# The last group of down products of a two-layer trunk, emitted from a written list: other places for weight blocks, additions and single residual tiles on VectorE

## The chip, the cores and the metric

The kernel runs on one core of one Trainium2 chip. The metric is the device time of one execution in microseconds (us); the time of the kernel before is the median of three runs. Durations and start times inside the kernel come from one profiled execution, whose own time and span are given below.

## What is computed

Two layers of a hybrid encoder on 512 tokens of width 1024, float32. Each layer is a token mixer (layer 0: differential attention, layer 1: chunked gated linear attention) with a memory cross-attention beside it, an output projection, and a gated MLP with a causal depthwise convolution. The change touches the end of the MLP, its down projection, and the way from there to the next layer:

```python
def conv_ffn(h, w_up, conv_w, conv_b, w_down):
    u = h @ w_up
    c = lax.conv_general_dilated(u, conv_w[:, None, :].astype(u.dtype), ...) + conv_b
    a, g = jnp.split(c, 2, axis=-1)
    return (jax.nn.silu(g) * a) @ w_down

for i in range(DEPTH):
    ...
    h = rms_norm(x, ffn_norm[i])
    x = x + conv_ffn(h, w_up[i], conv_w[i], conv_b[i], w_down[i])
```

The hidden width D_FF is 2816 and the output width 1024.

## The kernel before

**Number format.** Every float32 product is made of three matmuls: an operand is split into a high part (a cast) and a low part (the difference), and high x high, high x low and low x high are summed. For a weight block ScalarE makes the high part (tile whi) and VectorE the low part (tile wlo); there are five buffers of each (WB = 5). Raw weights arrive by DMA from SyncE's queue into six buffers.

**The down projection** runs in three groups of 3, 4 and 4 hidden blocks (`GROUPS`), each over two column halves c = 0, 1 of the output. It is a Winograd-like scheme of seven products instead of eight for a 2 x 2 block matrix: a11, s1, a12, s2, s4, s3, a22, where s1 to s4 are sums of weight blocks that VectorE forms (`sum_weights`, L251 to L264). `DOWN` (L34) lists the 14 products of a group in their order; I number them 0 to 13 by that list. Function `step` (L1161) emits one product on TensorE: 4 hidden blocks x 2 output tiles x 3 matmuls = 24 matmuls into one of the PSUM banks lg, tp, mm. Function `add` (L1179) follows: one VectorE addition of the bank onto two residual tiles, halved over tokens (t = 0 or 1). Products that go on in the same bank (for c = 0: a11, s2, s3, a22 in lg, and s1, s4 in tp) have to wait until the addition before has read it, since the bank is read as a running sum.

**Weight blocks.** `weights` (L305) hands out the next block of the plan. `prefetch(i)` (L298) makes all blocks that fit the five buffers when product i is the oldest one in use; with one product per step it makes one block. `make_sum` (L266) makes a block: the cast on ScalarE (L272), the weight sum that the next product needs (L251 to L264), and the low part on VectorE (L274). A block whose buffer is still being read waits for the step that reads it.

**Finished tiles.** `done(c, f, t)` (L1183) calls `finish` (L1236) for the two tiles of a pair once their additions are in. In layer 0 `finish` calls `settle` (L1071): ScalarE scales the tile into a high part (L315) and squares it (L429 or L1080), VectorE makes the low part (L318) and adds the square to a running sum (L431 or L1081); then the tile is stored to DRAM. For the last four tiles (n = 4 to 7) this is done by token halves. In layer 1 `finish` only stores the tile to the output.

**The last group** (L1194 to L1232) starts with the first three hidden blocks of products 0, 1 and 2, and adds the fourth block of each after that, because that hidden block is finished last.

**What comes after layer 0's group.** The first projection of layer 1's mixer (`gemm`, L329, called at L852; its weights are pieces gm0 and gm1 of 272 columns) takes the finished tiles in the order 0, 1, 2, 3, 6, 7, 4, 5 (`GM`, L38), token blocks 2 and 3 first, then 0 and 1. Between these two halves TensorE forms the sum of squares (L437), which needs all tiles, for the row scales of the layer. The weight blocks of the projection after it (g0) are made beside this.

**Who sets the order.** TensorE follows program order everywhere. Inside `down` (L1292) ScalarE, VectorE and GpSimd do too. Everything else, SyncE's queue among it, and the work before and behind `down`, is placed by the scheduler of the language, which can put such an instruction between two of the ordered ones. `follow` (L323) reads a written list like `ORDER` (L48): each entry is a letter, a number, and for some a bank, and calls the function of that letter.

Of the kernel before, what the change touches and what calls it, by code (L numbers as in the profile page):

```python
# [33 lines left out]
DOWN = ((0, "a11"), (0, "s1"), (0, "a12"), (0, "s2"), (0, "s4"), (0, "s3"), (1, "a11"), (0, "a22"),  # L34
        (1, "s1"), (1, "s2"), (1, "a12"), (1, "s3"), (1, "s4"), (1, "a22"))
K8 = tuple(range(KT))
C4 = tuple(range(4))
GM = (0, 1, 2, 3, 6, 7, 4, 5)  # L38

PASS = ([[(c, (0, 1, 2)) for c in C4], [(c, (3, 6, 7, 4, 5)) for c in C4]],  # L40
        [[(c, (0, 1, 2, 6, 7)) for c in (0, 1, 2)] + [(3, (0, 1, 2))],
         [(c, (3, 4, 5)) for c in (0, 1, 2)] + [(3, (6, 7, 3, 4, 5))]])
# [23 lines left out]
def _pieces():  # L66
# [3 lines left out]
    def piece(key, name, i, ks, *ranges):  # L70
        plan.append((key, name, i, ks, ranges))

    for l in range(2):
# [9 lines left out]
        else:  # L83
# [3 lines left out]
            for c in range(5):  # L87
                piece(("g", c), w, 0, K8, (512 * c, min(512 * c + 512, 2304)))
        for i, part in enumerate(PASS[l]):
            for c, ks in part:  # L90
# [69 lines left out]
def trunk(ctx, tc, head_d, x_t, mem_t, wpack, cols_a_d, cols_d, conv_d, gate_d, rel_bias, diff_lambda, consts, onehot, out):  # L160
    nc = tc.nc
    mm = nc.tensor.matmul
# [10 lines left out]
    def bank(tag):  # L173
        return ps.tile([128, 512], F32, name=f"ps_{tag}", tag=tag)
# [17 lines left out]
    def blk(b, w=128):  # L192
        return slice(w * b, w * b + w)
# [13 lines left out]
    def tables(name):  # L207
        tc.keep_in_program_order(A.preload_act_table_set(name))
# [71 lines left out]
    def make_piece(raws=None, between=None):  # L280
        key = plan[len(made)][0]
        if key[0] == "d":
            made.append(make_sum(key))
            return
        parts = []
        for i, (_, _, kk, _, w) in enumerate(blocks[len(made)]):
            n = len(kk)
            raw = load_raw(raw_tile(), n * w) if raws is None else raws[i]
            hi, lo = (wp.tile([128, WTILE], F32R, name=t, tag=t, bufs=WB) for t in ("whi", "wlo"))
            if between is not None and i == 3:  # L290
                between()
            split_weights(slice(0, n * w), raw, hi, lo, len(made) == 2)
            parts += [(hi[:, blk(j, w)], lo[:, blk(j, w)]) for j in range(n)]
        made.append(parts)
# [3 lines left out]
    def prefetch(i):  # L298
        size = lambda j: 1 if plan[j][0][0] == "d" else len(blocks[j])
        by_block = plan[i][0][0] in "ud"  # L300
        while len(made) <= i or (len(made) < len(plan) and (
                sum(map(size, range(i, len(made) + 1))) <= WB if by_block else len(made) < i + 2)):
            make_piece()
# [19 lines left out]
    def follow(order, steps):  # L323
        for entry in order.split():
            op, n, tag = entry[0], entry[1:].rstrip("tsl"), BANKS.get(entry[-1] if len(entry) > 1 else "")
            steps[op](int(n), **({} if tag is None else {"tag": tag}))
# [98 lines left out]
    first = [bank("mm"), bank("mm"), bank("sm"), bank("sm")]  # L425
# [24 lines left out]
    with tc.tile_pool(name="ini", bufs=1) as ip, tc.manual_schedule(engines={E.Activation, E.DVE, E.Pool, E.SP}):  # L450
# [7 lines left out]
        p = bank("tp")  # L458
# [45 lines left out]
        for k in range(KT):  # L504
# [15 lines left out]
            for b, i in sorted(todo, key=lambda bi: bi[1]) if k == 0 else todo:  # L520
                xp, w = terms[i]
# [562 lines left out]
    def out_proj(l, mix, part, acc, late=None):  # L1084
        got, kk = {}, dict(PASS[l][part])
        turns = cycle(("mm", "mm", "sm", "sm") if late is not None else ("mm", "sm") if acc else ("mm",))

        def unit(n, i):
            c, ks = n // 2, kk[n // 2]
            if i == 0:  # L1090
                if c not in got:
                    got[c] = weights(("o", l, part, c))
                got["p", n] = bank(next(turns))
            p = got["p", n]
            product(p, got[c], n % 2, [mix[k] for k in ks], (i,))
            if i == len(ks) - 1:
                update(n, p, None if acc is None else (lambda k: c_ffn(l, k)), acc)

        def give(units):
            for u in units:  # L1100
                F.add(0.65, lambda u=u: unit(*u))
        units = [(2 * c + n, i) for c, ks in PASS[l][part] for n in range(2) for i in range(len(ks))]
        if late is None:
# [5 lines left out]
    def ffn(pool, l, acc):  # L1109
# [47 lines left out]
        def down(g, mids, finish):  # L1157
            last, ks = len(mids) - 1, tuple(range(len(mids)))
            parts, banks, first, last_group = {}, {}, used[0], g + 1 == len(GROUPS)

            def step(c, tag, w, m, ks=ks, start=False, more=True):  # L1161
                if (c, w) not in parts:
                    parts[c, w] = weights(("d", l, g, c, w), more)
                elif more:
                    prefetch(first + more)
                if start:
                    banks[c, tag] = bank(tag)
                p = banks[c, tag]
                hi, lo = parts[c, w]
                for k in ks:  # L1170
                    mh, ml = mids[k][m]
                    for n in range(2):
                        o, ws = p[:, blk(n, 256)], slice(256 * k + 128 * n, 256 * k + 128 * n + 128)
                        terms = (hi, mh), (hi, ml), (lo, mh)
                        for i, (a, b) in enumerate(terms):
                            mm(o[:, ::-1], a[:, ws], b[:, ::-1], start=start and (k, n, i) == (0, 0, 0), stop=k == last and i == 2,  # L1176
                               skip_group_check=True)

            def add(c, tag, f, t):  # L1179
                x = xpair[2 * c + f][:, :, blk(t, 256)]  # L1180
                V.tensor_add(x, x, banks[c, tag].rearrange("p (n s) -> p n s", n=2))  # L1181

            def done(c, f, t=None):  # L1183
                for n in range(2):
                    finish(4 * c + 2 * f + n, t)
            if not last_group:
                step(0, "lg", "a11", "b11", start=True)
                add(0, "lg", 0, 0)
                step(0, "tp", "s1", "t1", start=True)
                add(0, "tp", 1, 1)  # L1190
                step(0, "mm", "a12", "b21", start=True)
                add(0, "mm", 0, 0)
            else:
                step(0, "lg", "a11", "b11", ks[:-1], True)  # L1194
                step(0, "tp", "s1", "t1", ks[:-1], True, False)
                step(0, "mm", "a12", "b21", ks[:-1], True, False)
                step(0, "lg", "a11", "b11", ks[-1:], more=False)
                add(0, "lg", 0, 0)
                step(0, "tp", "s1", "t1", ks[-1:], more=1)
                add(0, "tp", 1, 1)  # L1200
                step(0, "mm", "a12", "b21", ks[-1:], more=2)
                add(0, "mm", 0, 0)
            step(0, "lg", "s2", "t2")
            add(0, "lg", 0, 1)
            step(0, "tp", "s4", "b22")
            add(0, "tp", 0, 1)
            step(0, "lg", "s3", "t3")
            add(0, "lg", 1, 1)
            step(1, "lg", "a11", "b11", start=True)
            add(1, "lg", 0, 0)  # L1210
            step(0, "lg", "a22", "t4")
            add(0, "lg", 1, 0)
            done(0, 0)
            step(1, "tp", "s1", "t1", start=True)
            add(1, "tp", 1, 1)
            step(1, "lg", "s2", "t2")
            add(1, "lg", 0, 1)
            done(0, 1)
            if l == 0 and last_group:
                tables("natural_log_exp_and_others")  # L1220
            step(1, "mm", "a12", "b21", start=True)
            add(1, "mm", 0, 0)
            done(1, 0, 0)
            step(1, "lg", "s3", "t3")
            add(1, "lg", 1, 1)
            done(1, 1, 1)
            step(1, "tp", "s4", "b22")
            add(1, "tp", 0, 1)
            done(1, 0, 1)
            step(1, "lg", "a22", "t4")  # L1230
            add(1, "lg", 1, 0)
            done(1, 1, 0)  # L1232

        acc2, mids = [None], []

        def finish(n, t=None):  # L1236
            if l == 0:
                settle(n, lambda k: c_attn(1, k), acc2, t)
            if l and t is not None:
                nc.sync.dma_start(out[n][:, blk(t, S // 2)], xT[n][:, blk(t, S // 2)])  # L1240
            elif t is None or t == (n < 6):
                nc.sync.dma_start((out if l else xres)[n], xT[n])
# [28 lines left out]
        for what, i in _ffn():  # L1271
            if what == "up":
# [12 lines left out]
                if i % 2 == 0:  # L1285
                    w = pool.tile([128, 8, 256], F32, name="w", bufs=1)
# [3 lines left out]
            else:  # L1290
                n, last = GROUPS[i], i == len(GROUPS) - 1
# [6 lines left out]
    for l in range(2):  # L1298
        with tc.tile_pool(name=f"at{l}", bufs=2) as pool:
# [4 lines left out]
            else:  # L1304
                gla_layer(pool, mix, sums)
                out_proj(1, mix, len(PASS[1]) - 1, acc)
                F.flush()
# [77 lines left out]
```

## Time and profile before

| | us |
|---|---|
| median of 3 runs | 1160.02 (1159.99 to 1160.43) |
| the profiled execution | 1159.95 |
| its span | 1158.2 |
| last down group, layer 0, from its first matmul | 556.67 |
| sum of squares behind it (L437) | 605.45 |
| last down group, layer 1, from its first matmul | 1113.25 |
| last addition, layer 1 | 1154.26 |

Times in rows of the trace are microseconds from the span's start. A row of the timeline has the start, the duration, the engine, the line of the kernel, the operation, the output and inputs by name, shapes, the count of instructions merged in the row, and in brackets the idle time ahead of it with what ended it. PE is TensorE, PEld its weight loads, DVE VectorE, ACT ScalarE, POOL GpSimd, SP SyncE. Matmuls overlap in TensorE's pipeline, so a matmul's duration is longer than the distance to the next one.

### The profile page before, as it was taken

How to read it: one execution, taken by the hardware profiler on the slowest of the kernel's cores; microseconds unless marked ns; L12 is line 12 of the kernel's file. 1: busy time of each engine (PE TensorE's matmuls, PEld its weight loads, DVE VectorE, ACT ScalarE, POOL GpSimd, SP SyncE). 2: the span in 40 equal slices, each digit the busy share in tenths (PEclk: the TensorE clock that was granted, in tenths of full speed). 3: DMA queues.
4: the chain of work that ended last, by engine and by line, in shares of the span. 5: the costliest groups of instructions: out<-in, count | busy, mean ns of one | idle time of the engine just before them, and what ended most of it. 6: DMA issues, size and time to landing. Idle time of an engine off the chain costs nothing.

```text
span 1158.2 us, 16678 instructions
## 1 busy us (share of the span) xinstructions
PE 1146.7 (99%) x6448; PEld 986.5 (85%) x6448; DVE 884.1 (76%) x1450; ACT 596.9 (52%) x1035; POOL 4.1 (0%) x17
## 2 busy tenths in 40 slices
PE   9999999999999999999999999999999999999998
PEld 6888788888898889988997788988889988998888
DVE  7756768599896778578898656768998677876885
ACT  6846768466444444344467534436644344434441
POOL 0000000000000000000000000000000000000000
PEclk9999999999999999999999999999999999999999
DMA  9423232243135222522261221244222522252212
GB/s 311 159 80 120 69 128 59 75 128 96 55 106 163 92 73 74 164 92 73 66 198 67 74 73 46 85 144 126 74 65 71 194 91 74 73 164 92 73 37 74
DMA packets 39853, 117.94 MB, mean 102 GB/s; under 512 B 4735, under 2 KB 7608, under 8 KB 39774
## 3 DMA queue, kind: packets, MB, share of 16 engines
q1 hardware_dynamic: 39630, 116.62, 31.8%
q8 instruction: 51, 0.84, 0.3%
q14 instruction: 28, 0.23, 0.1%
q10 hardware_dynamic: 144, 0.26, 0.1%
HBM read 112.65 MB, written 4.21 MB: 101 GB/s over the span
## 4 chain that ended last, share of the span: by engine, by line
PE 88%; DVE 8%; ACT 2%; issue 1%; DMA 1%; DVEq 0%; ACTq 0%
PE ps_lg L1176 9%; PE ps_mm L364 9%; PE ps_mm L363 9%; PE ps_mm L365 9%; PE ps_sm L364 7%; PE ps_sm L363 7%; PE ps_sm L365 7%; PE ps_mm L342 5%; PE ps_mm L344 5%; PE ps_mm L343 5%; PE ps_tp L1176 4%; PE ps_mm L1176 2%; PE ps_tp L205 2%; DVE wlo L239 1%; PE ps_mm L522 1%; PE ps_lg L710 1%
## 5 line engine op out<-in xcount | busy, mean ns | idle before, releaser
L239 DVE TENSOR_TENSOR wlo<-raw,whi 128x1024 fp32r<-128x1024 f32 (+4 forms) x164 | 186.2, 1141 | 93.5 <-ACT whi L236 92.3
L236 ACT CAST whi<-raw 128x1024 fp32r<-128x1024 f32 (+4 forms) x164 | 160.6, 987 | 157.5 <-PE ps_sm L364 69.7
L363 PE MATMUL ps_mm<-x,whi 128*128 128x512 f32 x438 | 171.6, 392 | 0.4 <-DVE midh L1267 0.4
L364 PE MATMUL ps_mm<-x,whi 128*128 128x512 f32 x438 | 170.6, 389 | 0.2 <-DVE x L318 0.2
L365 PE MATMUL ps_mm<-x,wlo 128*128 128x512 f32 x438 | 170.5, 389 | 0.0
L363 PE MATMUL ps_sm<-x,whi 128*128 128x512 f32 x378 | 148.0, 391 | 0.0
L365 PE MATMUL ps_sm<-x,wlo 128*128 128x512 f32 x378 | 147.1, 389 | 0.0
L364 PE MATMUL ps_sm<-x,whi 128*128 128x512 f32 x378 | 147.1, 389 | 0.0
L342 PE MATMUL ps_mm<-whi,x 128*128 128x512 f32 (+2 forms) x336 | 129.8, 386 | 0.0
L344 PE MATMUL ps_mm<-whi,x 128*128 128x512 f32 (+2 forms) x336 | 126.3, 376 | 0.5 <-DVE x L318 0.4
L343 PE MATMUL ps_mm<-wlo,x 128*128 128x512 f32 (+2 forms) x336 | 125.9, 375 | 0.0
L272 ACT CAST whi<-raw 128x1024 fp32r<-128x1024 f32 (+1 forms) x60 | 58.4, 980 | 85.4 <-PE ps_sm L364 26.2
L363 PEld LDWEIGHTS ps_mm<-x,whi 128*128 128x128 f32 x438 | 82.3, 188 | 17.7 <-issue 0.7
L364 PEld LDWEIGHTS ps_mm<-x,whi 128*128 128x128 f32 x438 | 82.3, 188 | 17.2 <-DVE x L318 0.6
L365 PEld LDWEIGHTS ps_mm<-x,wlo 128*128 128x128 f32 x438 | 82.2, 188 | 17.1
L274 DVE TENSOR_TENSOR wlo<-raw,whi 128x1024 fp32r<-128x1024 f32 (+1 forms) x60 | 67.8, 1131 | 24.7 <-ACT whi L272 24.7
L363 PEld LDWEIGHTS ps_sm<-x,whi 128*128 128x128 f32 x378 | 71.0, 188 | 15.1 <-issue 0.5
L364 PEld LDWEIGHTS ps_sm<-x,whi 128*128 128x128 f32 x378 | 71.0, 188 | 14.9 <-issue 0.5
L365 PEld LDWEIGHTS ps_sm<-x,wlo 128*128 128x128 f32 x378 | 71.0, 188 | 14.7
L1176 PE MATMUL ps_lg<-midh,whi 128*128 128x256 f32 x264 | 74.8, 283 | 2.3 <-DVE x L1181 2.3
L1176 PE MATMUL ps_lg<-midh,wlo 128*128 128x256 f32 x264 | 74.3, 282 | 0.0
L1176 PE MATMUL ps_lg<-midl,whi 128*128 128x256 f32 x264 | 74.3, 281 | 0.0
(322 smaller groups left out, 2264.8 us busy)
## 6 DMA issues: line engine op xcount, KB each, us to landing
raw<-in_wpack_dram SPq DMA_DIRECT2D x170, 512.0 KB, 3.7
raw<-in_wpack_dram SPq DMA_DIRECT2D x24, 384.0 KB, 3.1
x<-in_x_t_dram SPq DMA_DIRECT2D x15, 256.0 KB, 4.8
xres<-x SPq DMA_DIRECT2D x8, 256.0 KB, 3.5
x<-xres SPq DMA_DIRECT2D x8, 256.0 KB, 4.8
raw<-in_wpack_dram SPq DMA_DIRECT2D x7, 256.0 KB, 5.4
bt<-bias_d SPq DMA_DIRECT2D x6, 256.0 KB, 3.5
x<-in_mem_t_dram SPq DMA_DIRECT2D x4, 256.0 KB, 6.0
```

Of the source, the lines that this page charges most:

```text
L205: nc.tensor.transpose(dst, src, ident[:n, :n])
L236: ins = A.copy(hi[:, c], raw[:, c])
L239: V.tensor_sub(lo[:, c], raw[:, c], hi[:, c].bitcast(F32))
L272: A.copy(hi[:, c], raw[:, c])
L274: todo = [lambda: V.tensor_sub(lo[:, c], raw[:, c], hi[:, c].bitcast(F32)), lambda: [sum_weights((*key[:3], *x)) for x in after]]
L342: mm(p, sh[k][:, blk(b)], hi, start=k == 0, stop=False)
L343: mm(p, sh[k][:, blk(b)], lo, start=False, stop=False)
L344: mm(p, sl[k][:, blk(b)], hi, start=False, stop=k == KT - 1)
L363: mm(p, hi[:, blk(n)], bh, start=i == first, stop=False)
L364: mm(p, hi[:, blk(n)], bl, start=False, stop=False)
L365: mm(p, lo[:, blk(n)], bh, start=False, stop=i == last)
L1176: mm(o[:, ::-1], a[:, ws], b[:, ::-1], start=start and (k, n, i) == (0, 0, 0), stop=k == last and i == 2, skip_group_check=True)
```

## The change

The emission of the last group is written as one list for each layer, `CLOSE`, and read by `follow`. The other groups go through `DOWN` in a loop, with the banks and residual places of `SEVEN`. Entries: `b` is a product's first hidden blocks, `e` its last one, `s` a whole product, `a` its addition, `p` a prefetch, `d` the finish of a whole tile, `h` that of a half tile (the tens digit is the token half, the units digit the tile), `t` the load of ScalarE's function table. Steps no longer prefetch themselves.

```diff
+SEVEN = {"a11": ("lg", "b11", 0, 0), "s1": ("tp", "t1", 1, 1), "a12": ("mm", "b21", 0, 0), "s2": ("lg", "t2", 0, 1),
+         "s4": ("tp", "b22", 0, 1), "s3": ("lg", "t3", 1, 1), "a22": ("lg", "t4", 1, 0)}
+CLOSE = ["""
+p0 b0 b1 b2 e0 a0 e1 a1 p3 p2 e2 a2 p1 s3 a3 s4 p4 a4 p5 s5 a5 p6 d0 s6 a6 p7 t0 s7 a7 p8 p9 d1 s8
+s9 a8 a9 d2 p10 d3 s10 a10 p11 s11 a11 h5 h4 h17 s12 a12 h16 p12 h14 h15 p13 s13 a13 h7 h6
+""", """
+p0 b0 b1 b2 e0 a0 p1 e1 a1 p2 e2 a2 p2 s3 a3 p3 s4 a4 p4 s5 a5 p5 s6 a6 p6 s7 a7 d0 d1 p7 s8 a8 p8
+s9 a9 d2 d3 p10 s10 a10 h4 h5 p11 s11 a11 h16 h17 p12 s12 a12 h14 h15 p13 s13 a13 h6 h7
+"""]
...
-            def step(c, tag, w, m, ks=ks, start=False, more=True):
+            def step(c, tag, w, m, ks=ks, start=False, more=False):
                 if (c, w) not in parts:
                     parts[c, w] = weights(("d", l, g, c, w), more)
-                elif more:
-                    prefetch(first + more)
...
             if not last_group:
...
+                for c, w in DOWN:
+                    tag, m, f, t = SEVEN[w]
+                    step(c, tag, w, m, start=w in ("a11", "s1", "a12"), more=True)
+                    add(c, tag, f, t)
+                return
+
+            def run(n, ks=ks):
+                c, w = DOWN[n]
+                step(c, SEVEN[w][0], w, SEVEN[w][1], ks, w in ("a11", "s1", "a12") and 0 in ks)
+
+            def sum_(n):
+                c, w = DOWN[n]
+                tag, _, f, t = SEVEN[w]
+                add(c, tag, f, t)
+            follow(CLOSE[l], dict(
+                s=run, b=lambda n: run(n, ks[:-1]), e=lambda n: run(n, ks[-1:]), a=sum_, p=lambda n: prefetch(first + n),
+                d=lambda n: finish(n), h=lambda n: finish(n % 10, n // 10), t=lambda n: tables("natural_log_exp_and_others")))
```

Written in the same letters, the order before was, in both layers (`t0` in layer 0 only):

```text
p0 b0 b1 b2 e0 a0 p1 e1 a1 p2 e2 a2 p3 s3 a3 p4 s4 a4 p5 s5 a5 p6 s6 a6 p7 s7 a7 d0 d1 p8 s8 a8 p9
s9 a9 d2 d3 t0 p10 s10 a10 h4 h5 p11 s11 a11 h16 h17 p12 s12 a12 h14 h15 p13 s13 a13 h6 h7
```

The order of the products on TensorE is the same in all three lists. Layer 1's list differs from the one before in its prefetches from `p3` on, which stand one product later up to block 13. Layer 0's list has blocks 5, 6 and 7 together ahead of the addition of product 2, blocks 12 and 13 together, the finished tiles one by one between other work, and the addition of product 11 directly behind that of product 10.

More of the change, by code (lines that the diff above doesn't have):

```diff
@@ L1181, in add @@
                 V.tensor_add(x, x, banks[c, tag].rearrange("p (n s) -> p n s", n=2))
-            def done(c, f, t=None):
-                for n in range(2):
-                    finish(4 * c + 2 * f + n, t)
             if not last_group:
[L1187 to L1231, printed above, removed]
@@ L1232, in down @@
-            done(1, 1, 0)
+                for c, w in DOWN:
[10 more added lines that the diff above has]
+                add(c, tag, f, t)
```

## The prediction

> **What bounds the kernel now.** I read the shares of the page first, then the waits of TensorE, then the two stretches that the change touches, row by row.
>
> ```profile
> PE 1146.7 (99%) x6448; PEld 986.5 (85%) x6448; DVE 884.1 (76%) x1450; ACT 596.9 (52%) x1035; POOL 4.1 (0%) x17
> PE ps_lg L1176 <- DVE x L1181: 2.3, 3, 1.0
> ```
>
> TensorE is busy 1146.7 of 1158.2 us, so the whole kernel can lose little more than 10 us by waiting less, and a reordering on VectorE can win only what TensorE waits in the last down group and right behind it. The second row (waits of TensorE) says that three down steps waited for an addition of L1181, 2.3 us in all. The next table gives the stretches, in this order: span, sum, then TensorE, weight loads, VectorE, ScalarE, GpSimd, clock, DMA.
>
> ```profile
> 563.80:571.70 7.90, 7.07 (x60) 6.86 (x58) 7.89 (x10) 4.36 (x5) 0.00 (x0) 1.00 0.18 53
> 571.70:591.60 19.90, 19.76 (x167) 19.79 (x168) 19.29 (x24) 11.77 (x15) 1.05 (x2) 1.00 0.54 168
> 591.60:605.50 13.90, 12.90 (x101) 12.07 (x99) 12.48 (x26) 9.61 (x21) 0.67 (x3) 1.00 0.55 179
> ```
>
> The reader is to see two things. In the first 8 us of layer 0's group VectorE is busy without a hole (7.89 of 7.90) while TensorE loses about 0.85 us; and VectorE stays full through 591.6 and still has 12.48 of 13.90 us at the end, where TensorE loses another microsecond. The clock is 1.00 throughout. These are TensorE's late starts, each with the matmul before it:
>
> ```profile
> 570.59 0.28 PE L1176 MATMUL ps_tp<-midh,wlo 128*128 128x256 f32 x1
> 571.84 0.36 PE L1176 MATMUL ps_lg<-midh,whi 128*128 128x256 f32 x1 [0.97 <-DVE x L1181]
> 594.51 0.28 PE L1176 MATMUL ps_tp<-midh,wlo 128*128 128x256 f32 x1
> 595.15 0.36 PE L1176 MATMUL ps_lg<-midh,whi 128*128 128x256 f32 x1 [0.35 <-DVE x L1181]
> 600.46 0.29 PE L343 MATMUL ps_mm<-wlo,x 128*128 128x272 f32 x1
> 601.19 0.39 PE L344 MATMUL ps_mm<-whi,x 128*128 128x272 f32 x1 [0.44 <-DVE x L318]
> 601.54 0.29 PE L343 MATMUL ps_mm<-wlo,x 128*128 128x272 f32 x1
> 601.92 0.40 PE L344 MATMUL ps_mm<-whi,x 128*128 128x272 f32 x1
> 605.04 0.29 PE L344 MATMUL ps_mm<-whi,x 128*128 128x272 f32 x1
> 605.45 0.72 PE L437 MATMUL ps_sm<-C,xt 128*128 128x1 f32 x5
> 1128.42 0.36 PE L1176 MATMUL ps_lg<-midh,whi 128*128 128x256 f32 x1 [0.97 <-DVE x L1181]
> 1137.18 2.84 PE ps_tp L1176 x24
> ```
>
> A step of 24 matmuls takes 2.84 us (last row, from the chain), that is 0.118 each, so a start 1.25 us after the one before (571.84) is 1.13 late; layer 1's at 1128.42 has the same idle time of 0.97 and should have been at 1127.29. After a stop the second matmul follows at 0.19 instead of 0.12, which adds 0.07. So either layer loses 1.20 at step 5 (s5, the second use of the bank lg, which must wait for a3), and layer 0 loses 0.59 at step 13, 0.60 + 0.10 at 601.19, 0.25 + 0.10 at 601.92 and 0.28 in front of L437, the sum of squares that the next layer's scales wait for (pitch of the 272-wide matmuls: 0.126, from 47 gaps between 598.07 and 605.04 less the two stops).
>
> **The change part by part.** TensorE's order, the matmuls, the additions, the weight blocks and the transfers are the same ones; no instruction is added or removed. The second p2 of layer 1, and p2 and p1 in layer 0, find their blocks made and issue nothing. What changes is VectorE's and ScalarE's order.
>
> *Layer 1, one block later.* The rows of VectorE around the stop, layer 1:
>
> ```profile
> 1124.73 0.68 DVE L1181 TENSOR_TENSOR x<-x,ps_mm 128x512 f32<-128x512 f32 x1
> 1125.33 1.22 DVE L256 TENSOR_TENSOR raws<-raw 128x1024 f32<-128x1024 f32 x1
> 1126.46 1.22 DVE L274 TENSOR_TENSOR wlo<-raw,whi 128x1024 fp32r<-128x1024 f32 x1
> 1127.60 0.68 DVE L1181 TENSOR_TENSOR x<-x,ps_lg 128x512 f32<-128x512 f32 x1
> ```
>
> In order: a2, the two operations of block 7, a3. The step that a3 reads (s3) ends one step (2.84) before 1127.29, plus TensorE's pipeline of some 0.15, at about 1124.6; a3 starts 3 us later only because block 7 (1.14 + 1.14 us from start to start) stands ahead of it. In the new list block 7 comes behind a3: a3 starts at 1125.33 and ends at 1126.0, and s5 can start at 1127.29, where s4 lets it. **Gain 1.20 us.** What is late next: block 7 is finished by 1128.3 and is needed at s7, 1132.97. Blocks 8 to 13 each slip by the one addition they now follow (0.60); carrying the sequence on with the same pitches, including a hole of 0.6 where ScalarE waits for a weight sum, gives a5 done at 1131.9 against 1132.97 for s7, block 8 at 1130.0 against 1135.8, and block 13 at 1143.5 against 1150.0 for s13. None is late. From there on TensorE ran without a stop already, and the tail (last addition, two last stores) keeps its length, so the end moves by the whole 1.20. The output stores wait on additions that come no later.
>
> *Layer 0, start of the group.* There block 5, 6 and 7 now stand together behind a1, and a2 and a3 behind them. Ahead of a3 stood a0, the late middle, block 5, a1, block 6, a2 and block 7; ahead of a3 stand the same eight operations now. So a3 stays at 571.02 to 571.70 and **the stop of 1.20 stays: gain 0**. Bounds: a1 may have to wait 0.1 for its step (minus 0.1), or the late middle may slide behind a3 (plus 0.87, its pitch), which s3's last quarter, needing it near 567, speaks against. Block 7's high part on ScalarE now stands ahead of everything that follows it there, as before.
>
> *Layer 0, tiles 0 to 3 (d0 to d3).*
>
> ```profile
> 578.34 1.05 ACT L272 CAST whi<-raw 128x1024 fp32r<-128x1024 f32 x1 [2.16 <-DVE raw L261]
> 579.29 0.72 ACT L315 ACTIVATE x<-x,cols_a 128x512 fp32r<-128x512 f32 x1
> 579.92 0.62 ACT L429 ACTIVATE xt<-x 128x512 f32<-128x512 f32 x1
> 587.55 0.68 DVE L1181 TENSOR_TENSOR x<-x,ps_lg 128x512 f32<-128x512 f32 x1
> ```
>
> They take the same time of VectorE in both orders. Ahead of a9 (last row), which s11 needs by about 588.95 (two steps of 2.84 before s13's 594.63), stood d0 and d1 and blocks 12 and 13; the same stand there now, so a9 stays at 587.55 and ends at 588.2. Nothing gained; margin about 0.6. ScalarE's half of d0 (0.72 and 0.62 in the rows) now falls into its hole of 2.16 before block 11, and the table load, d1 and d2 into others (it is busy 11.77 of 19.90); with that cover gone each would cost at most the 1.2 us that it takes.
>
> *Layer 0, the end.* Rows of VectorE, before:
>
> ```profile
> 591.59 0.68 DVE L1181 TENSOR_TENSOR x<-x,ps_mm 128x512 f32<-128x512 f32 x1
> 592.85 0.48 DVE L318 SCALAR_TENSOR_TENSOR x<-x,cols_a,x 128x256 fp32r<-128x256 f32 x1 [0.58 <-ACT x L315]
> 593.25 0.42 DVE L1081 TENSOR_TENSOR xt<-xt 128x256 f32<-128x256 f32 x1
> ...
> 594.32 0.68 DVE L1181 TENSOR_TENSOR x<-x,ps_lg 128x512 f32<-128x512 f32 x1
> ...
> 597.36 1.64 DVE L239 TENSOR_TENSOR wlo<-raw,whi 128x816 fp32r<-128x816 f32 x2 [0.23 <-ACT whi L236]
> 598.92 0.68 DVE L1181 TENSOR_TENSOR x<-x,ps_tp 128x512 f32<-128x512 f32 x1
> 599.52 1.22 DVE L239 TENSOR_TENSOR wlo<-raw,whi 128x1024 fp32r<-128x1024 f32 x1
> 600.65 0.48 DVE L318 SCALAR_TENSOR_TENSOR x<-x,cols_a,x 128x256 fp32r<-128x256 f32 x1
> ...
> 602.71 1.22 DVE L239 TENSOR_TENSOR wlo<-raw,whi 128x1024 fp32r<-128x1024 f32 x1
> ```
>
> Here a10, a11, a12 and a13 each stand ahead of their half tiles, and VectorE idles 0.58 while ScalarE makes the first of them. In the new list a11 follows a10 directly: it starts at 592.19 instead of 594.32 and ends at 592.9, and s13 (free to start at 594.63) no longer waits: **0.59**. The half tiles h5, h4, h17 (0.74 each: 0.40 + 0.34) fill the time to 595.07, when s12 is just over; a12 follows at 595.07 instead of 598.92, then h16, the two low parts of p12 (1.56) and h14 at 597.97, h15 at 598.71. The first projection of the next layer, which starts 0.59 earlier at 597.48, asks for h14's low half at 600.0 and for h15's at 600.4; they are there at 598.4 and 599.2: **0.70 and 0.35** go. L437 follows that projection at 603.53 (605.04 + 0.126 - 0.59 - 1.05) unless the last half tiles are later. VectorE: a13 at 599.45, h7 and h6 1.48 more with either the hole of 0.58 or the two weight parts (1.14 each) that the scheduler put into such holes before, so all is done between 602.1 and 603.8. L437 then starts between 603.53 and 603.85 instead of 605.45: 1.6 to 1.9 earlier, of which I take **1.8** in all (the 0.59 and 1.05 are in it).
>
> Everything behind L437 on its way through layer 1's mixer moves with it, as far as its order is kept. Sum: 1.20 + 0 + 1.8 = 3.0 us. The profiled execution took 1159.95 (span 1158.2 and 1.75 around it), so 1156.95; it lies 0.07 below the median, which gives **1157.0 us**.
>
> **A rule against it.** In layer 0, VectorE is busy 19.29 of 19.90 us, and its number of operations is the same before and after. The Trainium skill, "VectorE: DVE Perf Modes", section "The DRAIN you can't avoid" with its "Rules for kernel authors", says that the flush behind each operation happens however operations are chained, and that only their count helps; by that, a stretch bound by VectorE would keep its length. The trace bears it out for the full stretch up to 591.6 (1.22 us operations start 1.14 apart, without a hole), not behind it, where VectorE has 1.4 us of holes in 13.90.
>
> **Rivals.** (1) *VectorE stays the bound in layer 0.* If ScalarE's halves come as late as before, or more weight parts of the next layer are put ahead of the last half tiles, L437 keeps its 605.45; the work is the same and only 1.4 us of holes are to be had. Layer 1 alone gains: 1160.0 - 1.2 = 1158.8. For it: the full VectorE up to 591.6. Against: a11 and a12 are late behind work that nobody awaits yet. The rule above ends here. (2) *Layer 0's first stop goes too*, because the late middle goes behind a3: 1157.0 - 0.9 = 1156.1. (3) *The mixer is reordered.* Behind the list the scheduler places VectorE's and ScalarE's work itself, by times that the change shifts. There TensorE waits without slack for the softmax's scaling:
>
> ```profile
> PE ps_tp L205 <- DVE xt L613: 1.0, 3, 0.4
> 619.86 0.60 DVE xt L893
> 620.56 1.22 DVE gs L895
> ```
>
> If three more of the mixer's scans with their inputs (1.22 + 0.60 each) were put ahead of L613, it would come 5.5 us later; since the slack is nothing, every microsecond counts from the first, and the gain is eaten from 3.0 on: 1157.0 + 5.5 = 1162.5, slower than before. Against it: their inputs come in the same order as before. (4) *It makes no difference*: a stop appears elsewhere for each that goes; 1160.0.
>
> **How the numbers follow.** Forecast 0.60 (own range 1156.3 to 1157.8), rival 1 0.22, rival 2 0.06, rival 3 0.08, rival 4 0.04. A measurement of this kernel tells about 0.2% from no change: 2.3 us, so below 1157.7 is faster, above 1162.3 slower. Faster: 0.85 of the forecast and rival 2, 0.57. Slower: most of rival 3, 0.07. Within: 0.36. The range takes the forecast, rival 2 with its 0.87, and most of rival 1 with a few tenths of shift in the mixer: 1155.6 to 1159.4; left out are rivals 3 and 4 and the ends, about 0.17.
>
> **What would show it.** In layer 1's group no start of TensorE is late, and a3 stands directly behind a2. In layer 0 the late start of about 1.1 at the fifth step is still there; the one at the thirteenth and the two in the projection behind it are gone; L437 comes about 1.8 us earlier. It is wrong if L437 stays at its distance from the group's start (rival 1), if TensorE's waits for L613 grow (rival 3), or if a5 or a9, with 0.5 to 0.6 us to spare in layer 0, become late.

## The result and the profile after

The changed kernel takes 1156.83 us (median of 10 runs, 1156.37 to 1157.59) against 1160.24 us before (10 runs, 1159.46 to 1160.64): 3.41 us less, a ratio of 0.9972 with a 95% interval of 0.9962 to 0.9981. That is faster by 0.28%, with the interval clear of 1. The profiled execution took 1156.74 us, its span is 1154.9; before it was 1159.95 and 1158.2.

Lines of functions behind the new list have moved by 7 to 9: the additions L1181 are now L1188, the down matmuls L1176 are L1183, the sum of squares L437 is L446, the low parts L274 and L318 are L283 and L327.

First the page's busy times and the waits of TensorE for the additions, after:

```profile
PE 1145.6 (99%) x6448; PEld 986.3 (85%) x6448; DVE 884.1 (77%) x1450; ACT 596.5 (52%) x1035; POOL 4.1 (0%) x17
PE ps_lg L1183 <- DVE x L1188: 1.0, 1, 1.0
```

VectorE has the same 1450 instructions and the same 884.1 us as before. Of three late starts behind an addition one is left. The stretches of before, set at the same events in layer 0 (first addition to the end of a3, from there to a10, a10 to the sum of squares) and, in layer 1, from the first addition to a4, columns as before:

```profile
563.70:571.60 7.90, 7.07 (x60) 6.87 (x59) 7.89 (x10) 4.38 (x5) 0.00 (x0) 1.00 0.26 57
571.60:591.48 19.88, 19.73 (x167) 19.76 (x168) 19.28 (x24) 11.77 (x15) 1.05 (x2) 1.00 0.51 168
591.48:603.41 11.93, 11.93 (x100) 11.93 (x99) 11.93 (x25) 9.41 (x21) 1.15 (x3) 1.00 0.67 223
1118.36:1126.17 7.81, 7.81 (x68) 7.81 (x67) 7.81 (x9) 4.27 (x5) 0.00 (x0) 1.00 0.00 0
```

The first two rows are those of before to within 0.02 us: nothing was won there. The third shrank from 13.9 to 11.93 us, and in it TensorE and VectorE are both busy without a hole. In the fourth, layer 1, TensorE no longer loses anything. Before, it lost 0.85 us there, from the first addition to the end of a3:

```profile
1120.40:1128.30 7.90, 7.05 (x60) 6.84 (x58) 7.90 (x10) 4.35 (x5) 0.00 (x0) 1.00 0.00 0
```

The timeline of TensorE shows the same by its late starts: this is the only one left in the two groups, with the matmul before it, then the first matmul of layer 0's group, the sum of squares, and layer 1's first matmul:

```profile
570.49 0.28 PE L1183 MATMUL ps_tp<-midh,wlo 128*128 128x256 f32 x1
571.75 0.36 PE L1183 MATMUL ps_lg<-midh,whi 128*128 128x256 f32 x1 [0.97 <-DVE x L1188]
...
556.41 0.40 PE L1183 MATMUL ps_lg<-x,whi 128*128 128x256 f32 x2
603.41 0.95 PE L446 MATMUL ps_sm<-C,xt 128*128 128x1 f32 x8
1111.06 0.40 PE L1183 MATMUL ps_lg<-x,whi 128*128 128x256 f32 x2
```

I measure from here on by three distances: *group to squares* in layer 0 (603.41 - 556.41 = 47.00), *mixer* from the squares to layer 1's last group (507.65), and *last group* in layer 1, from its first matmul to its last addition. Before, the same rows of the timeline read 556.51, 605.45 and 1113.09 (the timeline has a group's first matmul 0.16 earlier than the chain, from which 556.67 and 1113.25 of the table of times before were read):

```profile
556.51 0.40 PE L1176 MATMUL ps_lg<-x,whi 128*128 128x256 f32 x2
1113.09 0.40 PE L1176 MATMUL ps_lg<-x,whi 128*128 128x256 f32 x2
```

| us | before | after | difference |
|---|---|---|---|
| span's start to layer 0's last group | 556.51 | 556.41 | -0.10 |
| group to squares | 48.94 | 47.00 | -1.94 |
| mixer and the rest of layer 1 | 507.64 | 507.65 | 0.0 |
| last group of layer 1 (to 1154.26 and 1151.02) | 41.17 | 39.96 | -1.21 |
| last addition to the span's end | 3.94 | 3.88 | -0.06 |

Distances are compared because the part ahead of layer 0's group, in which the kernels of the experiments do not differ from the changed one, took between 556.16 and 557.96 us in their profiled executions.

VectorE in layer 1, after, at the place where block 7 stood ahead of a3:

```profile
1122.70 0.68 DVE L1188 TENSOR_TENSOR x<-x,ps_mm 128x512 f32<-128x512 f32 x1
1123.30 0.68 DVE L1188 TENSOR_TENSOR x<-x,ps_lg 128x512 f32<-128x512 f32 x1
1123.90 1.22 DVE L265 TENSOR_TENSOR raws<-raw 128x1024 f32<-128x1024 f32 x1
1125.04 1.22 DVE L283 TENSOR_TENSOR wlo<-raw,whi 128x1024 fp32r<-128x1024 f32 x1
1126.17 0.68 DVE L1188 TENSOR_TENSOR x<-x,ps_tp 128x512 f32<-128x512 f32 x1
```

The two additions now follow each other, and the block's 2.27 us stand behind them. And the end of layer 0's group, after:

```profile
591.48 0.68 DVE L1188 TENSOR_TENSOR x<-x,ps_mm 128x512 f32<-128x512 f32 x1
592.08 0.68 DVE L1188 TENSOR_TENSOR x<-x,ps_lg 128x512 f32<-128x512 f32 x1
592.74 0.48 DVE L327 SCALAR_TENSOR_TENSOR x<-x,cols_a,x 128x256 fp32r<-128x256 f32 x1
...
594.95 0.68 DVE L1188 TENSOR_TENSOR x<-x,ps_tp 128x512 f32<-128x512 f32 x1
...
597.83 0.47 DVE L327 SCALAR_TENSOR_TENSOR x<-x,cols_a,x 128x256 fp32r<-128x256 f32 x1
...
599.29 0.68 DVE L1188 TENSOR_TENSOR x<-x,ps_lg 128x512 f32<-128x512 f32 x1
599.89 1.22 DVE L248 TENSOR_TENSOR wlo<-raw,whi 128x1024 fp32r<-128x1024 f32 x1
...
602.15 0.41 DVE L1090 TENSOR_TENSOR xt<-xt 128x256 f32<-128x256 f32 x1
602.49 1.22 DVE L248 TENSOR_TENSOR wlo<-raw,whi 128x1024 fp32r<-128x1024 f32 x1
```

a11 stands at 592.08 instead of 594.32, a12 at 594.95 instead of 598.92, and none of these rows has an idle time in brackets any more: the two holes of 0.58 and the one of 0.23 behind a10 are gone, since VectorE has other work while ScalarE prepares a half tile.

### The profile page after: what moved, and what is told of

Its sections match the earlier page's. It is cut to its first block, busy times and chain, and to the rows that moved or that the text cites. A ratio compares the mean times of both kernels' runs of the same rounds, so it can differ in the third digit from the quotient of the medians.

```text
span 1154.9 us, 16680 instructions
## 1 busy us (share of the span) xinstructions
PE 1145.6 (99%) x6448; PEld 986.3 (85%) x6448; DVE 884.1 (77%) x1450; ACT 596.5 (52%) x1035; POOL 4.1 (0%) x17
## 4 chain that ended last, share of the span: by engine, by line
PE 92%; DVE 5%; ACT 2%; issue 1%; DMA 0%; POOL 0%; DVEq 0%; ACTq 0%; POOLq 0%
PE ps_lg L1183 11%; PE ps_mm L373 9%; PE ps_mm L372 9%; PE ps_mm L374 9%; PE ps_sm L372 8%; PE ps_sm L373 8%; PE ps_sm L374 8%; PE ps_mm L351 5%; PE ps_tp L1183 5%; PE ps_mm L353 5%; PE ps_mm L352 5%; PE ps_mm L1183 3%; PE ps_tp L214 2%; PE ps_mm L531 1%; PE ps_lg L719 1%; PE ps_sm L531 1%
## 5 line engine op out<-in xcount | busy, mean ns | idle before, releaser
L283 DVE TENSOR_TENSOR wlo<-raw,whi 128x1024 fp32r<-128x1024 f32 (+1 forms) x60 | 67.7, 1132 | 24.8 <-ACT whi L281 24.8
L1183 PE MATMUL ps_lg<-midh,whi 128*128 128x256 f32 x264 | 74.7, 283 | 1.0 <-DVE x L1188 1.0
L1183 PE MATMUL ps_lg<-midl,whi 128*128 128x256 f32 x264 | 74.3, 282 | 0.0
L1183 PE MATMUL ps_lg<-midh,wlo 128*128 128x256 f32 x264 | 74.3, 282 | 0.0
```

Of the source, the lines that this page charges most:

```text
L283: todo = [lambda: V.tensor_sub(lo[:, c], raw[:, c], hi[:, c].bitcast(F32)), lambda: [sum_weights((*key[:3], *x)) for x in after]]
```

## The experiments

The theory under test is that of **queue places**: VectorE works in order, and a start of TensorE is late when the addition or half tile that it waits for stands behind work that nobody awaits yet. The first rival is that VectorE is simply **full** in layer 0, so that only the count of its operations sets the length there. Others are named with each run. All kernels but e5 differ from the changed one by entries of the lists alone.

### Each layer's list alone

`e1_layer1_only` has the old list in layer 0, `e2_layer0_only` the old one in layer 1. Written short, for e1, with "old" and "new" for the lists of before and after:

```diff
-CLOSE = [new 0, new 1]
+CLOSE = [old 0, new 1]
```

> Layer 0 keeps the old list, layer 1 has the new one. Theory of queue places (each late start of TensorE goes when the addition it waits for stands ahead of work that nobody awaits yet): the start of s5 in layer 1 is not late, 1.2 us of the 3.4 are won, about 1159.0 us, ratio 0.9990. Rival (VectorE is the bound, only its count of operations sets the length): no gain, 1160.2. Layer 0 shows its late starts as before: 1.1 at s5, 0.5 at s13, 0.6 and 0.3 in the projection behind.

> Layer 0 has the new list, layer 1 the old one. Theory of queue places: the sum of squares behind the group comes 1.9 us earlier after the group's first matmul (46.8 instead of 48.8 us), about 1158.2 us, ratio 0.9983, and layer 1's s5 is 1.1 late as before. The two gains add: 1.2 and 1.9 to 2.1 make the 3.4 of the whole change. Rival (VectorE bound in layer 0): nothing, 1160.2.

Measured: e1 1158.88 us, ratio 0.9987 (0.9979 to 0.9996), 1.3 us under its runs of before; e2 1158.33 us, 0.9982 (0.9973 to 0.9991), 1.9 under. Together 3.2 of the 3.4. In e1 the group to squares is 48.94 as before, in e2 47.00; e2's layer 1 has its late start back:

```profile
1126.21 0.36 PE L1183 MATMUL ps_lg<-midh,whi 128*128 128x256 f32 x1 [0.98 <-DVE x L1188]
```

So the gains belong to the two lists separately and add up, and the rival that layer 0 has nothing to give is out.

### Layer 1: one swap instead of the whole shift

```diff
-... e2 a2 p2 s3 a3 p3 s4 a4 p4 s5 a5 p5 ...
+... e2 a2 s3 a3 p3 p4 s4 a4 p5 s5 a5 p6 ...
```

> Layer 0 new; layer 1 has the old list with one swap alone: a3 ahead of block 7, blocks 8 to 13 at their old places. Theory of queue places: s5 starts on time (1.2 won), but a5 stands behind the same work as before and ends when it did, about 20.4 us after the group's first matmul, while s7 could start at 19.7; s7 is then 0.7 to 0.9 late and only 0.3 to 0.5 of the 1.2 remain: about 1157.8 us. Rival (one late addition was all that was wrong, the rest of the shift is idle): the whole 1.2, 1156.8 us.

Measured: 1158.01 us, ratio 0.9981 (0.9972 to 0.9990); layer 1's last group takes 41.01 (1111.38 to 1152.39), only 0.16 less than with the old list. TensorE and VectorE in this kernel:

```profile
1132.23 0.36 PE L1183 MATMUL ps_lg<-midh,whi 128*128 128x256 f32 x1 [0.82 <-DVE x L1188]
```

```profile
1123.62 0.68 DVE L1188 TENSOR_TENSOR x<-x,ps_lg 128x512 f32<-128x512 f32 x1
1124.21 1.22 DVE L265 TENSOR_TENSOR raws<-raw 128x1024 f32<-128x1024 f32 x1
...
1131.41 0.68 DVE L1188 TENSOR_TENSOR x<-x,ps_lg 128x512 f32<-128x512 f32 x1
```

a3 comes early at 1123.62, s5 is on time, and then s7 starts 0.97 late, because a5 (last row) stands behind the same work as ever and ends at 1132.09. The stop has moved by two steps instead of going. A single early addition is worth almost nothing here; the additions behind it have to come one block earlier too, which is what the new list does. I had expected 0.3 to 0.5 to remain; it was 0.16, since the late start is 0.97 plus the slower restart of 0.07 and not 0.7 to 0.9.

### Layer 0: front or end of the list

`e6_old_end` has the new list up to d3 and the old one from product 10 on; `e7_new_end` the old one up to the table load and the new one from there; both have layer 1's new list.

```diff
-old: ... s10 a10 h4 h5 p11 s11 a11 h16 h17 p12 s12 a12 h14 h15 p13 s13 a13 h6 h7
+e7: ... s10 a10 p11 s11 a11 h5 h4 h17 s12 a12 h16 p12 h14 h15 p13 s13 a13 h7 h6
```

> Layer 1 new; layer 0 has the new list up to d3 and the old one from product 10 on. Theory (the gain of layer 0 lies in its end alone): the sum of squares is back at 48.8 us after the group's first matmul, total about 1158.9 us as with layer 1's list alone. Rival (blocks 5 to 7 together and the finished tiles one by one win something themselves): between 1156.8 and 1158.9.

> Layer 1 new; layer 0 has the old list up to the table load and the new one from product 10 on. Theory (the gain lies in the end alone): 46.8 us from the group's first matmul to the sum of squares, total 1156.8 us, all of the change's gain, with the start of s5 1.1 late as before. Rival (the front part matters): up to 1158.9.

Measured: e6 1158.92 us, ratio 0.9989 (0.9980 to 0.9997), group to squares 48.94; e7 1156.78 us, ratio 0.9968 (0.9955 to 0.9980), group to squares 46.99. (e6's profiled execution took 1160.25 us, 1.3 above the median; its group starts at 557.96, 1.5 us later than in the changed kernel, and its distances from there on are not touched by that.) The end alone makes all of the 1.94. Blocks 5 to 7 together, blocks 12 and 13 together, and the single tiles d0 to d3 win nothing and lose nothing.

### Layer 0: one addition moved

```diff
-e1: ... s10 a10 h4 h5 p11 s11 a11 h16 h17 p12 s12 a12 h14 h15 ...
+e9: ... s10 a10 p11 s11 a11 h4 h5 h16 h17 p12 s12 a12 h14 h15 ...
```

> Layer 1 new; layer 0 has the old list with one edit: a11 directly behind a10, ahead of h4 and h5. Theory of queue places: s13 is on time, and VectorE loses one of its holes of 0.6, so a12 also comes at about 597.3 instead of 598.9 (with the group at 556.6), h14's low half is there in time for the projection, and the last half tile at about 603.8: 1.6 to 1.8 of the 1.9 us of layer 0, total about 1157.2 us. Rival (each late start is a term by itself, and the two in the projection belong to a12's place): only 0.6, about 1158.3 us.

Measured: 1157.40 us, ratio 0.9976 (0.9966 to 0.9986); group to squares 604.03 - 556.40 = 47.63, 1.31 of the 1.94. The place of a11 is thus most of the gain and not the 0.6 of one late start; a12 came 1.3 us earlier, counted from the group's start, without being moved itself. Less than expected, because two small late starts of TensorE stayed, one in the projection and one at the sum of squares (each with the matmul before it; behind them VectorE's rows):

```profile
600.13 0.29 PE L352 MATMUL ps_mm<-wlo,x 128*128 128x272 f32 x1
600.50 0.39 PE L353 MATMUL ps_mm<-whi,x 128*128 128x272 f32 x1
603.61 0.29 PE L353 MATMUL ps_mm<-whi,x 128*128 128x272 f32 x1
604.03 1.05 PE L446 MATMUL ps_sm<-C,xt 128*128 128x1 f32 x8
```

```profile
597.50 0.68 DVE L1188 TENSOR_TENSOR x<-x,ps_tp 128x512 f32<-128x512 f32 x1
598.09 1.22 DVE L248 TENSOR_TENSOR wlo<-raw,whi 128x1024 fp32r<-128x1024 f32 x1
599.23 0.48 DVE L327 SCALAR_TENSOR_TENSOR x<-x,cols_a,x 128x256 fp32r<-128x256 f32 x1
...
603.56 0.42 DVE L1090 TENSOR_TENSOR xt<-xt 128x256 f32<-128x256 f32 x1
```

Between a12 and its half tile the scheduler put a weight part of the next projection (598.09), and another ahead of the last two half tiles. In the changed kernel a12 comes early enough that only one such part falls ahead of the last half tile. By the pitch of 0.126 the two starts are 0.25 and 0.29 late, and the first restart costs 0.10: together the remaining 0.6. Which of the list's other moves behind a10 (h16, p12, the order of the half tiles) wins how much of it, no run separates.

### Layer 0: the stop that the change left

`e4_both_early` gives layer 0 the shift of layer 1, with d0 ahead of block 9, where VectorE has a hole; d1 moves behind a9, and p11 is left out.

```diff
-p0 b0 b1 b2 e0 a0 e1 a1 p3 p2 e2 a2 p1 s3 a3 s4 p4 a4 p5 s5 a5 p6 d0 s6 a6 p7 t0 s7 a7 p8 p9 d1 s8
-s9 a8 a9 d2 p10 d3 s10 a10 p11 s11 a11 h5 ...
+p0 b0 b1 b2 e0 a0 p1 e1 a1 p2 e2 a2 s3 a3 p3 s4 a4 p4 s5 a5 d0 p5 s6 a6 p6 t0 s7 a7 p7 s8 a8 p8 p9
+s9 a9 d1 d2 p10 d3 s10 a10 s11 a11 h5 ...
```

> Layer 1 new; layer 0 with the blocks shifted behind the additions as in layer 1 from p3 on, d0 ahead of block 9 (in the hole where VectorE waits for ScalarE), and the new end from d1 on. Theory of queue places: a3 ends at about 569.3 instead of 571.6, s5 in layer 0 is on time, a5 is done at 575.2 against 576.3 for s7, a9 at 586.2 against 587.6 for s11, a11 at 592.0 against 593.3 for s13, and the last half tile at 601.9 against 602.2 for the sum of squares: the remaining 1.2 us go, about 1155.6 us. Rival (VectorE full in layer 0, what is won at s5 is given back at s7, s11 or the sum of squares): 1156.8.

Measured: 1156.40 us, ratio 0.9966 (0.9952 to 0.9979), 0.4 under the changed kernel instead of 1.2. The two sets of runs overlap (1156.14 to 1156.82 and 1156.37 to 1157.59), so the reading rests on the distances in the trace. Neither side is right as it stands. The group to squares is 602.02 - 556.24 = 45.78: the 1.22 are won, with no late start of TensorE in the group. But the mixer takes 508.47 instead of 507.65. ScalarE there:

```profile
623.19 1.28 ACT L217 ACT_TABLE_LOAD   x1
624.48 1.28 ACT L901 ACT_TABLE_LOAD   x1
625.77 0.63 ACT L901 ACTIVATE xt<-xt 96x512 f32<-96x512 f32 x1
...
627.14 1.28 ACT L618 ACT_TABLE_LOAD   x1
```

```profile
630.53 0.63 PE L214 MATMUL ps_tp<-C,xt 128*128 128x128 f32 x4 [1.21 <-DVE xt L622]
```

With the new times the scheduler placed the load of the exp table (623.19) ahead of the last Ln of the gates, L901, which needs the other table: ScalarE loads that one back and the exp table once more. TensorE waits 1.21 us for the softmax's scaling instead of 0.41. This is the prediction's third rival, in small and on another engine than the one it priced. `e5_early_table` is e4 with the last Ln and the load kept in order:

```diff
-            A.activation(t, t, AF.Ln, bias=1.0)
+            if h < 3:
+                A.activation(t, t, AF.Ln, bias=1.0)
+            else:
+                with tc.manual_schedule(engines={E.Activation}):
+                    A.activation(t, t, AF.Ln, bias=1.0)
+                    tables("exp_and_others")
...
-        tables("exp_and_others")
```

> The kernel of e4_both_early with the last Ln of the gates and the load of the exp table held in program order on ScalarE. In e4 the sum of squares came 1.2 us earlier as expected, but the scheduler put the load of the exp table ahead of the last Ln, so that ScalarE loaded the table twice more (1.28 us each), and TensorE waited 1.2 us instead of 0.4 for the softmax's scaling. Theory: with the two loads gone the 0.75 us come back, about 1155.6 us, ratio 0.9960. Rival (the mixer simply has its own length from some later point, whatever the loads): 1156.4.

Measured: **1155.19 us** (1154.73 to 1155.30), ratio 0.9953 (0.9939 to 0.9966), the fastest here and 1.6 us under the changed kernel. ScalarE loads the table once, and the exponentials start in time:

```profile
624.30 0.63 ACT L905 ACTIVATE xt<-xt 96x512 f32<-96x512 f32 x1
624.95 1.28 ACT L217 ACT_TABLE_LOAD   x1
...
627.52 0.47 ACT L618 ACTIVATE xt<-ps_lg,nmm 128x256 f32<-128x256 f32 x1 [0.72 <-DVE nmm L614]
```

The squares are at 602.80 here, so the first exponential comes 24.7 us behind them; in the changed kernel it was 25.7 (629.08 and 603.41). The mixer is 506.73 long: not only e4's 0.8 came back, but the 0.9 that TensorE lost around its first two waits for L622 in the changed kernel. The expectation, 1155.6, had only the former. The group to squares is 45.78 as in e4; since the group starts at 557.02 in this execution, 0.6 later than in the changed kernel's, the span shows 1.5 of the 2.1 us that the two distances are shorter.

## Why the prediction was right

1157.0 was forecast, 1156.83 measured. The forecast takes 3.0 us off 1160.02; the two distances that the change shortened give 1.94 + 1.21 = 3.15. The rest of the 3.41 is 0.16 ahead of layer 0's group and behind the last addition, 0.01 back in the mixer, and the difference between medians and profiled executions, none of which was forecast. By its steps:

- **Layer 1, 1.20:** measured 1.21. a3 stands directly behind a2 as said, no start of TensorE is late, a5 and the later blocks are in time. e3 shows that the slip of blocks 8 to 13 by one addition each, none of them late, carried the gain, and not the swap of a3 and block 7 alone. (In bank lg, s5 is the third product, behind 0 and 3, not the second as the prediction counts; that it waits for a3 is right.)
- **Layer 0's first stop stays, 0:** measured 0; the late start is there, 0.97 as before. The argument, the same eight operations ahead of a3, held to 0.1 us (a3 0.1 earlier on the clock, like the group). e4 takes that stop away by changing which operations stand there.
- **Tiles d0 to d3, 0:** e7, without the new places, has the same group to squares.
- **The end of layer 0, 1.8:** measured 1.94. The bound that I worked out from TensorE alone, 603.53 with the group at 556.51, was reached (603.41 with the group at 556.41). I had taken a middle value because of the two weight parts that the scheduler might put ahead of the last half tile; it put one there. As a sum of terms (0.59, 0.70, 0.35, 0.28) the step is right for the whole; e9 shows that the terms are not independent, since a11's place alone pulls a12 forward.
- **The mixer moves along, 0:** measured 0.0 in the changed kernel. That was not safe: e4, which differs from it in a dozen places of one list, lost 0.8 there.
- **The rule against the change**, that only the count of VectorE's operations helps (the Trainium skill, "VectorE: DVE Perf Modes", section "Rules for kernel authors"), was not tested where the prediction lets it stand. The stretch from a3 to a10 is 19.88 us long after and 19.90 before, but that is the length of seven steps of TensorE (7 x 2.84 = 19.88), which runs through it, and not a length that VectorE sets. Nor is VectorE there "without a hole", as the prediction reads it: it waits 0.58 ahead of block 9, before (first row) and after (second row):

```profile
575.27 1.22 DVE L274 TENSOR_TENSOR wlo<-raws,whi 128x1024 fp32r<-128x1024 f32 x1 [0.58 <-ACT whi L272]
575.16 1.23 DVE L283 TENSOR_TENSOR wlo<-raws,whi 128x1024 fp32r<-128x1024 f32 x1 [0.57 <-ACT whi L281]
```

Where VectorE has no hole, in the first 8 us of the group, e4 takes TensorE's stop away by the order of the operations, with as many of them in the kernel (1450); and behind a10 the list's operations stayed the same and 1.94 us went. So count alone did not set the length at either place.

What decided for 0.3% was slack that could be read beforehand: each addition's place in the queue, and the step that needs it.

## What to carry to other kernels

Where TensorE waits for an engine that works in order, list the operations ahead of the awaited one and ask of each when its own result is needed; what is needed later goes behind, and everything after it has to be checked again, since one swap can simply move the stop two steps on (e3). Fill the queue of one engine while another prepares its next operand: three holes, 1.39 us together (0.58, 0.58 and 0.23), stood in the stretch that became 1.94 shorter. And when a scheduler places the work around a hand-made order, look at that work again after each edit, function table loads first.

## What was not expected

Three table loads where one was needed cost ScalarE 2.56 us more, but the mixer only 0.8 against the changed kernel, and 1.74 against e5 (508.47 and 506.73). And the first two waits for the softmax's scaling, 0.39 and 0.29 us before and 0.41 and 0.28 in the changed kernel, are gone in e5. The place of the table load does not explain that, for in the changed kernel, too, the load stands directly behind the last Ln. These are ScalarE's rows there:

```profile
623.33 0.20 ACT L942 ACTIVATE e<-hb 96x4 f32<-96x4 f32 x1 [0.72 <-DVE hb L935]
...
625.58 0.62 ACT L901 ACTIVATE xt<-xt 96x512 f32<-96x512 f32 x1
626.22 1.28 ACT L217 ACT_TABLE_LOAD   x1
...
629.08 0.47 ACT L618 ACTIVATE xt<-ps_lg,nmm 128x256 f32<-128x256 f32 x1 [0.39 <-DVE nmm L614]
```

The exponentials (L618) wait for the maxima (nmm), which VectorE takes behind its last scan of the gates, and that scan needs the last Ln. In e5 the last Ln starts 21.50 us behind the squares instead of 22.17, and the maxima start 24.03 behind them instead of 24.95. One of the things that changed is the small exponential of the first row, on which ScalarE waits 0.72 us: in e5 it stands behind the load. So this looks like a queue place again, but e5 moved several operations at once, and no run moves this one alone.
